# Attention weights kept by key block and multiplied with V once per pair of heads; the memory normalised next to the last pair

## The chip, the core and the metric

The kernel runs on one core of one Trainium2 chip. The metric is the device time of one execution in microseconds (us). The engines of the core are named as in the profile: PE (the tensor engine's products), PEld (its weight loads), DVE (the vector engine), ACT (the scalar engine), POOL (GpSimd) and SP (the engine that issues most of the transfers).

## The reference

One layer of a decoder over 512 tokens of width 1024: a projection, two kinds of causal attention with 8 heads of 64 each, an output projection, cross attention to 256 memory tokens, a mixture of 16 experts, and a norm. What matters here:

```python
u = rmsnorm(h)
qA, kA, vA, qB, kB, vB, f = split(u @ w_in)
# FoX: per head, causal softmax with a decay from the forget gates
p = softmax(mask(qA @ kA.T / 8 + c_t - c_s));            oA = p @ vA
# stick-breaking: per head, strictly causal
a = exp(logsigmoid(z) + sum_{s<j<t} logsigmoid(-z_tj));  oB = a @ vB     # z = qB @ kB.T / 8
h = h + concat(rmsnorm(oA), rmsnorm(oB)) @ w_out
kv = rmsnorm(mem) @ w_xkv          # 256 memory tokens
h = h + cross_attention(rmsnorm(h) @ w_xq, kv) @ w_xo
```

## The kernel before

The tokens come last first, so a block of 128 queries sees its own block of keys and those behind it: query block i has 4 - i key blocks, in all 10 blocks of 128 x 128 for a head. Heads are handled in pairs, four pairs for each of the two families: FoX (`fox_pair`, group 0) and stick-breaking (`sb_pair`, group 1). Within a pair, three groups of query blocks, `BLOCKS = ((0,), (1, 3), (2,))`, are gone through head by head.

For each head and group, PE multiplies Q and K (`products`, into the PSUM tile `lg` for FoX, of which there is one, or `Z` for stick-breaking, of which there are two), ACT and DVE make the weights (tiles `p` or `sa`), PE transposes them block by block into the one PSUM tile `tr` (`transposed`), and DVE (FoX) or ACT (stick-breaking, as the exponential) copies `tr` to SBUF as `pT`. When both heads of the group are there, `av` multiplies them with V: for each key block and head one float32 product of 64 columns of V with 128 queries. The two heads write the upper and lower half of the PSUM tile `o`, side by side in the columns of the tensor engine. After the last group `pair_out` copies `o` to its place in `HO` and adds its squares for the norm that follows (`sq`).

The steps of the two families take turns. The projections of the next pair's Q and K (`qk_proj`) and of further V columns (`v_proj`) are written behind the steps of a pair; they read the normalised input as `uh` and `ul`, in three products each (`mm3`). Weights for them come through a ring of three raw tiles, which ACT casts (`wh`) and DVE subtracts from (`wl`). Q and K are then moved into the tiles QQ, KH, KL, QX and KX by transfers on SP.

The order of the instructions on each engine is fixed when the program is built, by a scheduler that moves instructions of later code between those of earlier code where it expects an engine to be free. On the chip each engine goes through its own list in order and waits at semaphores.

The memory (256 tokens) is loaded, normalised (`rms`), transposed and split into `mh` and `ml` (`to_fm`) behind the first V projections, before the first pair; the four rounds of its transpositions rotate over four PSUM tiles (`tr`, `lg` and two `o`). Its keys, products `pj<-mh`, are written behind the last pair, and the scheduler uses them there to fill PE.

Of the kernel before, what the change touches and what calls it, by code (L numbers as in the profile page):

```python
# [11 lines left out]
F32 = mybir.dt.float32  # L12
# [23 lines left out]
FIRST = 4  # L36


def layer(ctx, tc, a, out, dbg=None):
# [24 lines left out]
    # ---------------------------------------------------------------- helpers  # L64
    # a weight unit is 1024 values a partition: loaded whole, then split into two float32r parts
    W = {}

    # the places of a weight's tiles, in turn: (pool, tag count) for the raw unit and for its parts
# [71 lines left out]
    # -------------------------------------------------------------- constants  # L140
# [17 lines left out]
    # ================================================= phase 1: projection, FoX, SB  # L158
# [27 lines left out]
    mp = pool(ckm, "mp", side="left")  # L186
    mh = mp.tile([128, KT, M], F32R, name="mh")
    ml = mp.tile([128, KT, M], F32R, name="ml")
# [13 lines left out]
    # ---- forget gates  # L202
# [20 lines left out]
    # ---- pieces  # L223
# [82 lines left out]
    # what the heads give, by feature: the heads of a pair share a tile  # L306
# [3 lines left out]
    # the tokens come last first: the keys of a query block are its own block and those behind it;  # L310
    # the products of a pair's heads run side by side in the columns of the tensor engine
    def av(o, i, at, pTs, vcol):
        for s in range(i, NT):
            for hh in range(2):
                nc.tensor.matmul(o[hh * HD:(hh + 1) * HD, i * 128:(i + 1) * 128],  # L315
                                 V[:, s, vcol + hh * HD:vcol + (hh + 1) * HD], pTs[hh][:, at + s - i, :],
                                 start=s == i, stop=s == NT - 1)

    def transposed(p, w, copy):
        pt = trp.tile([128, NT, 128], F32, name="tr")  # L320
        for s in range(w // 128):
            nc.tensor.transpose(pt[:, s, :], p[:, s * 128:(s + 1) * 128], ident)  # L322
        pT = wk.tile([128, NT, 128], F32, name="pT", bufs=6)
        copy(pT[:, :w // 128, :], pt[:, :w // 128, :])
        return pT

    # blocks of queries that are handled together
# [16 lines left out]
    # the features of a pair of heads go to their place; their squares are summed over the pairs  # L344
# [9 lines left out]
    def fox_pair(p, ops):  # L354
        o = op_.tile([128, S], F32, name="o4", bufs=2)
# [971 lines left out]
```

## Time and profile before

| | |
|---|---|
| median of 3 runs | 664.81 us (664.63 to 665.65) |
| profiled execution, first to last instruction | 662.1 us |
| PE busy | 625.6 us |
| DVE busy | 461.6 us |
| ACT busy | 376.7 us |
| mean granted clock of PE | 0.990 of full speed |

The span of 662.1 us is that of one profiled execution; the times of the runs hold in addition what lies around the span, some 2.7 us at the median. Busy times of an engine are those of its instructions; matmuls are pipelined, so what a product costs PE is read from the start of one to the start of the next. In the profile of this execution the attention of the four pairs begins at about 69, 112, 177 and 220 us, and two V projections stand between the second and the third pair.

### The profile page before, as it was taken

What the parts mean: (1) busy time and instruction counts of PE and PEld (TensorE: products, weight loads), DVE (VectorE), ACT (ScalarE), POOL (GpSimd) and SP (SyncE); (2) the same over time, 40 slices, a digit from 0 to 9 for tenths busy, and PEclk for the clock granted to TensorE, in tenths of its full rate; (3) what the DMA queues carried; (4) which work ended last, traced back from release to release, by engine and by line L of the source; (5) the groups of instructions that cost most, each with busy time, mean ns of one, the idle gap of its engine ahead of it and who ended that gap; (6) DMA issues with size and microseconds to landing.
All of it is one profiled execution on the core that took longest, in us unless ns stands there. A gap on an engine that the chain in (4) does not pass through costs nothing.

```text
span 662.1 us, 10336 instructions
## 1 busy us (share of the span) xinstructions
PE 625.6 (94%) x3595; PEld 507.4 (77%) x3596; DVE 461.6 (70%) x941; ACT 376.7 (57%) x752; POOL 53.1 (8%) x80
## 2 busy tenths in 40 slices
PE   3999999999999999999999999999999999999980
PEld 2988777888877888988888898867767777777750
DVE  4843794963497797855853466347879999989955
ACT  5632556653456676613632354333369898898842
POOL 2000000000000000000000003000152011010350
PEclk9999999999999999999999999999999999999996
DMA  8545744323764634561453223792989999999494
GB/s 279 171 125 133 186 113 116 92 65 92 171 157 107 169 104 152 200 218 35 121 166 96 77 84 88 260 367 99 313 258 366 378 388 380 386 383 385 130 201 174
DMA packets 105497, 128.91 MB, mean 195 GB/s; under 512 B 8456, under 2 KB 82240, under 8 KB 105440
## 3 DMA queue, kind: packets, MB, share of 16 engines
q1 hardware_dynamic: 101120, 114.43, 54.8%
q0 software_dynamic: 4320, 13.77, 7.6%
q8 instruction: 29, 0.48, 0.3%
q14 instruction: 28, 0.23, 0.1%
HBM read 103.96 MB, written 11.56 MB: 174 GB/s over the span
## 4 chain that ended last, share of the span: by engine, by line
PE 82%; DMA 6%; DVE 4%; ACT 3%; issue 2%; POOL 1%; SPq 1%; DVEq 0%; POOLq 0%
PE pj L136 8%; PE pj L138 8%; PE pj L137 8%; PE o L315 5%; PE gu L136 4%; PE pja L136 4%; PE gu L137 4%; PE gu L138 4%; PE pja L137 4%; PE pja L138 4%; PE tr L322 3%; PE tr L129 3%; PE pjb L137 3%; PE pjb L136 3%; PE pjb L138 3%; PE dn L136 2%
## 5 line engine op out<-in xcount | busy, mean ns | idle before, releaser
L90 DVE TENSOR_TENSOR wl<-w,wh 128x1024 fp32r<-128x1024 f32 (+1 forms) x64 | 78.3, 1223 | 81.3 <-ACT wh L89 75.1
L89 ACT CAST wh<-w 128x1024 fp32r<-128x1024 f32 (+1 forms) x64 | 67.2, 1050 | 104.5 <-PE pj L137 37.3
L709 DVE TENSOR_TENSOR wl<-w,wh 128x512 fp32r<-128x512 f32 x168 | 108.5, 686 | 5.5 <-ACT wh L708 5.1
L708 ACT CAST wh<-w 128x512 fp32r<-128x512 f32 x168 | 96.6, 621 | 12.8 <-PE gu L138 9.8
L136 PE MATMUL pj<-uh,wh 128*128 128x512 f32 x128 | 52.1, 407 | 0.0
L138 PE MATMUL pj<-uh,wl 128*128 128x512 f32 x128 | 51.5, 403 | 0.0
L137 PE MATMUL pj<-ul,wh 128*128 128x512 f32 x128 | 51.2, 400 | 0.0
L136 PE MATMUL gu<-wh,xh 128*128 128x512 f32 x120 | 48.5, 404 | 0.2 <-ACT xh L131 0.2
L138 PE MATMUL gu<-wh,xl 128*128 128x512 f32 x120 | 47.6, 397 | 0.0
L137 PE MATMUL gu<-wl,xh 128*128 128x512 f32 x120 | 47.1, 393 | 0.0
L136 PE MATMUL pj<-wh,uh 128*128 128x256 f32 (+1 forms) x128 | 37.7, 294 | 2.3 <-ACT uh L131 2.3
L138 PE MATMUL pj<-wh,ul 128*128 128x256 f32 (+1 forms) x128 | 37.5, 293 | 0.0
L137 PE MATMUL pj<-wl,uh 128*128 128x256 f32 (+1 forms) x128 | 37.3, 292 | 0.0
L315 PE MATMUL o<-pT,V 128*64 128x128 f32 x320 | 33.0, 284 | 0.1
L136 PE MATMUL pja<-wh,fmh 128*128 128x512 f32 x80 | 32.4, 405 | 0.0
L137 PE MATMUL pja<-wl,fmh 128*128 128x512 f32 x80 | 31.9, 399 | 0.0
L138 PE MATMUL pja<-wh,fml 128*128 128x512 f32 x80 | 31.8, 398 | 0.0
L315 PEld LDWEIGHTS o<-pT,V 128*64 128x64 f32 x320 | 21.4, 136 | 10.0 <-issue 5.2
L136 PEld LDWEIGHTS pj<-uh,wh 128*128 128x128 f32 x128 | 24.1, 188 | 6.3 <-issue 1.7
L138 PEld LDWEIGHTS pj<-uh,wl 128*128 128x128 f32 x128 | 24.1, 188 | 5.9 <-issue 0.9
L368 ACT ACTIVATE p<-lg,nm 128x512 f32<-128x512 f32 (+3 forms) x32 | 16.9, 527 | 20.4 <-DVE nm L366 20.3
L137 PEld LDWEIGHTS pj<-ul,wh 128*128 128x128 f32 x128 | 24.1, 188 | 4.8 <-issue 0.3
(356 smaller groups left out, 1633.2 us busy)
## 6 DMA issues: line engine op xcount, KB each, us to landing
w<-in_w_exp_gate_dram SPq DMA_DIRECT2D x64, 256.0 KB, 7.6
w<-in_w_exp_up_dram SPq DMA_DIRECT2D x64, 256.0 KB, 7.6
w<-in_w_exp_down_dram SPq DMA_DIRECT2D x32, 512.0 KB, 7.6
w<-in_w_in_dram SPq DMA_DIRECT2D x24, 512.0 KB, 4.1
w<-in_w_xkv_dram SPq DMA_DIRECT2D x16, 512.0 KB, 4.4
Y<-y SPq DMA_DIRECT2D x14, 512.0 KB, 8.7
KH<-th SPq DMA_DIRECT2D x32, 128.0 KB, 2.3
w<-in_w_out_dram SPq DMA_DIRECT2D x8, 512.0 KB, 4.3
```

The source lines that it names most:

```text
L89: nc.scalar.copy(h, raw)
L90: nc.vector.tensor_sub(l, raw, h)
L129: nc.tensor.transpose(pt[:, j, :], src[:, k * 128:(k + 1) * 128], ident)
L136: nc.tensor.matmul(o, lh, rh, start=start, stop=False)
L137: nc.tensor.matmul(o, lh, rl, start=False, stop=False)
L138: nc.tensor.matmul(o, ll, rh, start=False, stop=stop)
L315: nc.tensor.matmul(o[hh * HD:(hh + 1) * HD, i * 128:(i + 1) * 128], V[:, s, vcol + hh * HD:vcol + (hh + 1) * HD], pTs[hh][:, at + s - i, : ...
L322: nc.tensor.transpose(pt[:, s, :], p[:, s * 128:(s + 1) * 128], ident)
L368: nc.scalar.activation(p_[:, cs], lg[:, cs], AF.Exp, bias=nm, scale=1.0, accum_out=sm)
L708: nc.scalar.copy(h, raw)
L709: nc.vector.tensor_sub(l, raw, h)
```

## The change

`av` is called once for a pair and family, when all groups of both heads are done. The copies of the transposed weights go into one tile of 15 blocks for each head, in which the query blocks of a key block stand next to each other. `av` then goes through five runs of (key block, first query block, number of query blocks): 384, 128, 384, 256 and 128 columns. The generators leave the weights in `W`, and the loop multiplies both families and calls `pair_out` after the last step of a pair. `pT` gets 4 tiles of 15 blocks instead of 6 of 4 blocks.

The memory's load, norm and transposition become a function that is called behind the projections of the last pair, after the pool of `uh` and `ul` is closed: `mh`, `ml` and the tiles of its norm take the place of `uh` and `ul`. All its transpositions go through `trp`, which has one tile. Its gain is loaded on POOL's queue instead of SP's. Otherwise comments are taken out, which shifts lines.

```diff
+PTS = 4
...
     ckm = ExitStack()
-    mp = pool(ckm, "mp", side="left")
-    mh = mp.tile([128, KT, M], F32R, name="mh")
-    ml = mp.tile([128, KT, M], F32R, name="ml")
     cu = ExitStack()
...
-    def av(o, i, at, pTs, vcol):
-        for s in range(i, NT):
-            for hh in range(2):
-                nc.tensor.matmul(o[hh * HD:(hh + 1) * HD, i * 128:(i + 1) * 128],
-                                 V[:, s, vcol + hh * HD:vcol + (hh + 1) * HD], pTs[hh][:, at + s - i, :],
-                                 start=s == i, stop=s == NT - 1)
-
-    def transposed(p, w, copy):
+    def av(pTs, vcol):
+        o = op_.tile([128, S], F32, name="o4", bufs=2)
+        runs = [(NT - 1, 0, NT - 1, 3 * NT - 3), (NT - 1, NT - 1, 1, 3 * NT + 1)]
+        runs += [(s, 0, s + 1, 3 * s) for s in range(NT - 2, -1, -1)]
+        for n, (s, i, w, at) in enumerate(runs):
+            for hh in (1, 0):
+                nc.tensor.matmul(o[hh * HD:(hh + 1) * HD, i * 128:(i + w) * 128],
+                                 V[:, s, vcol + hh * HD:vcol + (hh + 1) * HD],
+                                 pTs[hh][:, at * 128:(at + w) * 128],
+                                 start=n == 0, stop=n == len(runs) - 1, skip_group_check=True)
+        return o
+
+    def transposed(p, at, w, pT, copy):
         pt = trp.tile([128, NT, 128], F32, name="tr")
         for s in range(w // 128):
             nc.tensor.transpose(pt[:, s, :], p[:, s * 128:(s + 1) * 128], ident)
-        pT = wk.tile([128, NT, 128], F32, name="pT", bufs=6)
-        copy(pT[:, :w // 128, :], pt[:, :w // 128, :])
-        return pT
+        i = at[0][0]
+        n = w // 128
+        dst = pT.rearrange("p (a b q) -> p a b q", b=3, q=128)[:, :, i % 3, :]
+        copy(dst[:, i + i // 3:i + i // 3 + n, :], pt[:, :n, :])
+
+    def weights_by_key():
+        return [wk.tile([128, 15 * 128], F32, name="pT", bufs=PTS) for _ in range(2)]
...
     def fox_pair(p, ops):
-        o = op_.tile([128, S], F32, name="o4", bufs=2)
+        pTs = weights_by_key()
...
-                pTs.append(transposed(p_, w, nc.vector.tensor_copy))
-                if len(pTs) == 1:
-                    yield
-            for i, cs in at:
-                av(o, i, cs.start // 128, pTs, p * 128)
-            yield
-        pair_out(o, 0, p)
+                transposed(p_, at, w, pTs[hh], nc.vector.tensor_copy)
+                yield
+        W["av0"] = pTs
...
-    mark("mem")
-    g_mem = nw.tile([128, D], F32, name="gain", bufs=2)
-    nc.sync.dma_start(g_mem, a["norm_mem"][0].partition_broadcast(128))
-    for t in range(2):
-        xt = nw.tile([128, D], F32, name="mt", bufs=2)
-        nc.sync.dma_start(xt, mem2[t * 128:(t + 1) * 128, :])
-        rms(nw, xt, g_mem, xt, D)
-        to_fm(src, xt, mh, ml, t * 128)
     cn.close()
-    qk = pool(c1, "qk", side="right")
-    wk = pool(c1, "wk", side="right")
+
+    def memory():
+        mp = pool(ckm, "mp", side="left")
+        mh, ml = (mp.tile([128, KT, M], F32R, name=n) for n in ("mh", "ml"))
+        with ExitStack() as cm:
+            mw = pool(cm, "mw", side="left")
+            g_mem = gain_bc(mw, a["norm_mem"][0], D, 1)
+            for t in range(2):
+                xt = mw.tile([128, D], F32, name="mt", bufs=2)
+                nc.sync.dma_start(xt, mem2[t * 128:(t + 1) * 128, :])
+                rms(mw, xt, g_mem, xt, D)
+                to_fm(trp, xt, mh, ml, t * 128)
+        return mh, ml
+
+    ca = ExitStack()
+    qk = pool(ca, "qk", side="right")
+    wk = pool(ca, "wk", side="right")
...
         for c in "sf":
             for _ in steps[c]:
                 pass
+
+        for g in range(2):
+            pair_out(av(W[f"av{g}"], g * 512 + p * 128), g, p)
...
             nb = qk_proj(1, p + 1)
             na = qk_proj(0, p + 1)
-    cu.close()
-
-    # ================================================= memory keys and values
+        if p == 2:
+            cu.close()
+            mh, ml = memory()
+
+    ca.close()
```

The same edit as in `fox_pair` is made in `sb_pair`, with `exp` as the copy and `W["av1"]`.

How the instructions stand on the engines, in the program as it is built (a line, an operation, output <- inputs, the output's size; `x4` is four in a row). First PE at the end of the third pair before, where the last transpositions and V products stand between projection products (`pj<-uh`):

```order
L137 MATMUL pj<-ul,wh 128x512
L138 MATMUL pj<-uh,wl 128x512
L322 MATMUL tr<-ident,sa 128x128 x2
L315 MATMUL o_1978<-pT,V 64x128
L136 MATMUL pj<-uh,wh 128x512
L137 MATMUL pj<-ul,wh 128x512
L315 MATMUL o_1958<-pT,V 64x128 x3
L322 MATMUL tr<-ident,p 128x128 x2
L138 MATMUL pj<-uh,wl 128x512
L136 MATMUL pj<-uh,wh 128x512
L137 MATMUL pj<-ul,wh 128x512
L315 MATMUL o_1978<-pT,V 64x128 x3
```

And PE there in the change, from the last two transpositions on; ahead of them the projection products have run out:

```order
L327 MATMUL tr<-ident,sa 128x128 x2
L327 MATMUL tr<-ident,p 128x128 x2
L318 MATMUL o_2077<-pT,V 64x384 x2
L318 MATMUL o_2077<-pT,V 64x128 x2
L318 MATMUL o_2077<-pT,V 64x384 x2
L318 MATMUL o_2077<-pT,V 64x256 x2
L318 MATMUL o_2077<-pT,V 64x128 x2
L318 MATMUL o_2092<-pT,V 64x384 x2
L318 MATMUL o_2092<-pT,V 64x128 x2
L318 MATMUL o_2092<-pT,V 64x384 x2
L318 MATMUL o_2092<-pT,V 64x256 x2
L318 MATMUL o_2092<-pT,V 64x128 x2
```

The V products of both families have moved from many places into one piece of 20. The second place is PE at the beginning of the last pair. Before, the products with the memory (`pj<-mh`) follow the pair's first Z products directly:

```order
L138 MATMUL pj<-uh,wl 128x512
L341 MATMUL Z<-KH,QQ 128x512
L341 MATMUL Z<-KL,QQ 128x512
L341 MATMUL Z<-KH,QQ 128x512
L341 MATMUL Z<-KL,QQ 128x512
L136 MATMUL pj<-mh,wh 128x256
L137 MATMUL pj<-ml,wh 128x256
L138 MATMUL pj<-mh,wl 128x256
```

In the change these come behind the V products, the logits of the next groups and the transpositions of the memory (`mt`):

```order
L350 MATMUL Z<-KH,QQ 128x384
L350 MATMUL Z<-KL,QQ 128x384
L350 MATMUL Z<-KH,QQ 128x128
L350 MATMUL Z<-KL,QQ 128x128
L130 MATMUL tr<-ident,mt 128x128 x12
L350 MATMUL Z<-KH,QQ 128x256
L350 MATMUL Z<-KL,QQ 128x256
L137 MATMUL pj<-mh,wh 128x256 x2
L130 MATMUL tr<-ident,mt 128x128 x4
L138 MATMUL pj<-ml,wh 128x256
L139 MATMUL pj<-mh,wl 128x256
L350 MATMUL lg<-KH,QQ 128x384
```

The memory's transpositions, which stood before the first pair, now stand between PE and its fill. The third place is ACT at the same point. Before, behind the copies and squares of the third pair's two outputs:

```order
L346 COPY HO<-o_1958 128x512
L351 ACTIVATE sa<-o_1958 128x512
L346 COPY HO<-o_1978 128x512
L351 ACTIVATE sa<-o_1978 128x512
L89 CAST wh<-w 128x1024
L279 CAST th<-pj 128x512
L397 ACTIVATE sa<-Z 128x512
```

And in the change; `junk,ss<-mt` is the memory's sum of squares:

```order
L355 COPY HO<-o_2077 128x512
L360 ACTIVATE sa<-o_2077 128x512
L355 COPY HO<-o_2092 128x512
L360 ACTIVATE sa<-o_2092 128x512
L400 ACTIVATE sa<-Z 128x512
L401 ACTIVATE sa<-sa 128x512
L376 ACTIVATE p,sm<-lg,nm 128x512
L402 ACTIVATE sa<-sa 128x512
L400 ACTIVATE sa<-Z 128x512
L401 ACTIVATE sa<-sa 128x512
L402 ACTIVATE sa<-sa 128x512
L116 ACTIVATE junk,ss<-mt 128x1024
```

The memory's norm has moved in between the first operations of the last pair.

## Rows read from the trace of the kernel before

**Rows 1.** The page, busy time of each engine in us, share of the span, and instructions.

```profile
PE 625.6 (94%) x3595; PEld 507.4 (77%) x3596; DVE 461.6 (70%) x941; ACT 376.7 (57%) x752; POOL 53.1 (8%) x80
```

**Rows 2.** Busy time by stage: the attention of the first pair and of the third, each from its first Z product to its last V product. Start and end, length, then busy us (and instructions) of PE, PEld, DVE, ACT, POOL, the granted clock, and the transfers.

```profile
68.66:108.40 39.74, 39.24 (x237) 28.91 (x235) 32.46 (x72) 24.77 (x52) 0.00 (x0) 1.00 0.56 140
177.40:217.20 39.80, 39.22 (x237) 28.89 (x235) 32.92 (x73) 24.74 (x52) 0.00 (x0) 1.00 0.57 137
```

**Rows 3.** The line of the V products: records, duration in ns (least, median, most), first and last start.

```profile
L315 PE MATMUL o<-pT,V x320: 272/273/324, 76.1 to 259.9; 128*64 128x128 f32 x160
```

**Rows 4.** PE in order of time in the first pair's attention: start, duration, line, operation, count.

```profile
81.58 0.43 PE L315 MATMUL o<-pT,V 128*64 128x128 f32 x2
81.94 0.50 PE L136 MATMUL pj<-uh,wh 128*128 128x512 f32 x1
82.28 0.39 PE L137 MATMUL pj<-ul,wh 128*128 128x512 f32 x1
82.51 0.40 PE L138 MATMUL pj<-uh,wl 128*128 128x512 f32 x1
82.84 1.09 PE L315 MATMUL o<-pT,V 128*64 128x128 f32 x14
83.86 0.50 PE L136 MATMUL pj<-uh,wh 128*128 128x512 f32 x1
84.19 0.39 PE L137 MATMUL pj<-ul,wh 128*128 128x512 f32 x1
```

**Rows 5.** The chain of work that ended last: start, us on the chain, what. The first of these rows is four transpositions of the memory.

```profile
42.18 0.44 PE tr L129 x4
...
82.91 1.02 PE o L315 x14
...
106.20 0.58 PE o L315 x6
```

**Rows 6.** PE in order of time between the third pair and the last.

```profile
220.07 0.39 PE L138 MATMUL pj<-uh,wl 128*128 128x512 f32 x1
...
221.00 0.39 PE L341 MATMUL Z<-KL,QQ 128*128 128x512 f32 x1
221.23 0.28 PE L136 MATMUL pj<-mh,wh 128*128 128x256 f32 x1
```

**Rows 7.** Instructions of DVE and ACT by line and shape from 220.3 to 240 us (count, busy us, mean ns of one, idle time before them), and two neighbours on DVE in order of time.

```profile
L400 DVE SCALAR_TENSOR_TENSOR sa<-Z,sa 128x512 f32<-128x512 f32 x4 | 2.7, 686 | 0.4 <-ACT sa L399 0.3
L403 DVE TENSOR_TENSOR_SCAN sa<-sa 128x512 f32<-128x512 f32 x2 | 2.4, 1220 | 0.0
L403 DVE TENSOR_TENSOR_SCAN sa<-sa 128x384 f32<-128x384 f32 x2 | 1.9, 948 | 0.0
L404 DVE TENSOR_TENSOR sa<-Z,sa 128x512 f32<-128x512 f32 x3 | 2.1, 684 | 0.0
L395 DVE TENSOR_TENSOR Z<-Z,negs 128x128 f32<-128x128 f32 x6 | 1.7, 286 | 1.9 <-PE Z L341 1.9
L366 DVE TENSOR_REDUCE nm<-lg 128x1 f32<-128x512 f32 x2 | 1.4, 681 | 0.0
L398 ACT ACTIVATE sa<-sa 128x512 f32<-128x512 f32 x4 | 2.5, 631 | 0.1
...
203.59 0.68 DVE L280 TENSOR_TENSOR tl<-pj,th 128x512 fp32r<-128x512 f32 x1
204.19 0.15 DVE L370 RECIPROCAL rs<-sm 128x1 f32<-128x1 f32 x1
```

**Rows 8.** The memory's multiplication by the norm and its remainder `ml` on DVE and its square on ACT, by line and shape from 24 to 48 us, and its transpositions on PE in order of time, from the first to the product behind them.

```profile
L117 DVE SCALAR_TENSOR_TENSOR mt<-mt,rr,gain 128x1024 f32<-128x1024 f32 x2 | 2.6, 1288 | 0.1
L131 DVE TENSOR_TENSOR ml<-o,mh 128x512 fp32r<-128x512 f32 x2 | 1.3, 680 | 0.0
L115 ACT ACTIVATE junk<-mt 128x1024 bf16<-128x1024 f32 x2 | 2.1, 1054 | 0.0
...
42.02 0.60 PE L129 MATMUL tr<-ident,mt 128*128 128x128 f32 x4
...
43.68 0.48 PE L136 MATMUL pj<-uh,wh 128*128 128x512 f32 x1
```

**Rows 9.** Moves of K on SP in order of time at the last pair, and from the issues of transfers (count, KB each, median us to landing) the weights for the memory and the memory itself.

```profile
223.71 1.24 SPq L303 DMA_DIRECT2D KH<-th  x2
...
w<-in_w_xkv_dram SPq DMA_DIRECT2D x16, 512.0 KB, 4.4
mt<-in_mem_dram SPq DMA_DIRECT2D x2, 512.0 KB, 6.3
```

**Rows 10.** PE in order of time near the start, and busy time by stage near the end (columns as in rows 2; the granted clock is the third number from the end).

```profile
15.49 0.41 PE L136 MATMUL pj<-wh,uh 128*128 128x256 f32 x1
15.70 0.41 PE L137 MATMUL pj<-wl,uh 128*128 128x256 f32 x1
...
17.83 0.28 PE L138 MATMUL pj<-wh,ul 128*128 128x256 f32 x1
17.95 0.28 PE L136 MATMUL pj<-wh,uh 128*128 128x256 f32 x1
...
646.00:647.00 1.00, 0.07 (x1) 0.00 (x0) 1.00 (x4) 0.53 (x1) 0.00 (x0) 1.00 0.98 279
650.00:651.00 1.00, 0.00 (x0) 0.00 (x0) 1.00 (x5) 0.05 (x1) 0.00 (x0) 0.50 0.00 0
```

More of the change, by code (lines that the diff above doesn't have):

```diff
@@ L354, in fox_pair @@
     def fox_pair(p, ops):
-        o = op_.tile([128, S], F32, name="o4", bufs=2)
+        pTs = weights_by_key()
         for blocks in BLOCKS:
             at, w = spans(blocks)
-            pTs = []
-            for Q, K in ops:
+            for hh, (Q, K) in enumerate(ops):
                 lg = lgp.tile([128, S], F32, name="lg", bufs=1)
@@ L386, in sb_pair @@
     def sb_pair(p, ops):
-        o = op_.tile([128, S], F32, name="o4", bufs=2)
+        pTs = weights_by_key()
         for blocks in BLOCKS:
             at, w = spans(blocks)
-            pTs = []
-            for Q, K in ops:
+            for hh, (Q, K) in enumerate(ops):
                 z = zp.tile([128, S], F32, name="Z", bufs=2)
@@ L404, in sb_pair @@
                 nc.vector.tensor_sub(c[:, :w], z[:, :w], c[:, :w])
-                pTs.append(transposed(c, w, exp))
-                if len(pTs) == 1:
-                    yield
-            for i, cs in at:
-                av(o, i, cs.start // 128, pTs, 512 + p * 128)
-            yield
-        pair_out(o, 1, p)
+                transposed(c, at, w, pTs[hh], exp)
+                yield
+        W["av1"] = pTs
     cn = ExitStack()
```

## The prediction

> **What bounds the kernel now.** I read the page first, then the busy time of the engines by stage, then the tensor engine's instructions in order of time. The page says that PE is busy for 625.6 of 662.1 us [rows 1]. The stages in which the change works look the same: in the attention of the first and of the third pair, PE is busy 39.24 of 39.74 us and 39.22 of 39.80, and DVE 32.46 and 32.92 [rows 2]. So PE is the bound, a microsecond that PE loses or wins there is one of the kernel, and DVE is not far behind. What PE does per microsecond is read from start to start, since matmuls overlap: a product of 512 columns comes every 0.23 us [rows 4].
>
> **What the V products cost now.** They are 320 records [rows 3], two for each of 160 products. The order of before cuts them into 48 pieces: for each pair, family and block group first one product alone (one head, 2 records), later the remaining 7 (14 records) or 3 (6 records). That is 24 pieces of 2, 16 of 14 and 8 of 6. A piece costs more than its products: around the one at 82.84, PE goes from 82.51 to 84.19, which is 1.68 us with two projection products in it that are worth 0.47, so the piece costs 1.21 [rows 4]. The chain of waits gives it 1.02 and a piece of six 0.58 [rows 5]; entering and leaving thus adds 0.19. A piece of two takes 0.36 (81.58 to 81.94), with its ends 0.55. In all 24 x 0.55 + 16 x 1.21 + 8 x 0.77 = 38.8 us of PE time.
>
> **What they cost after.** The columns that stream are the same. 1.02 less 0.58 is 0.44 us for eight more records, that is 0.11 us for two: the records of the two heads, which sit in different halves of the array's columns, run side by side; one record alone takes 0.11 too, as a transposition does [rows 5]. Walking the new order (widths 384, 128, 384, 256, 128, each for both heads, records starting in order, a head's own one after the other) gives 2.7 us for one family and 5.3 for both, because a narrow product waits behind the other head's wide one. Full overlap would give 4.4, none 8.7. The new order puts all 20 products of a pair in one piece, so with its ends 5.6, and 22.4 us for four pairs. **Gain: 38.8 - 22.4 = 16.4 us**; the bounds are 20 and 2.6. The page "TensorEngine Tiling (Array Packing)" of the Trainium skill (Theoretical Speedup) promises up to 2x for an operand of 64 columns; by it the piece would be 4.6 and the gain 20 us. The present pieces reach 1.75x (seven products in eight steps), so I keep the walk. The copies into the weights by key move as many elements in equal runs of 128, so I cost them at nothing.
>
> **What moving the memory costs.** Before, loads, squares and splits of the memory lie beside projection products, and its 16 transpositions take 1.66 us in a row, in four PSUM tiles, without a wait [rows 8]. After, its tiles lie where uh and ul lay, so nothing of it can start before the last product that reads them; its transpositions share the one `tr` tile; and the key products of the memory (`pj<-mh`), which fill PE from 221.23 on [rows 6], wait for it. I walk this stretch with t = 0 where the last product with uh ends (220.30 before).
>
> - 0 to 4.3: PE has the next pair's four Z products and six transpositions. The last three rounds of these pass through the one `tr` tile, each with a copy by ACT or DVE, and ACT casts a weight unit (1.05) between; the last copy ends at about 4.2.
> - 4.3 to 9.8: the V products. 9.7 to 10.2: the first FoX logits of the last pair.
> - ACT has the results of both families (copy, square, copy, square) ahead of the last pair's first stick-breaking operation; the second copy waits for 9.8, so that operation starts at about 10.9, although its input was there at 1.3. Before, the same order stood there, but PE had products to go on with.
> - From 10.4 DVE has 41 instructions up to the third remainder `ml`: four like L400, scans of 512 x2, 384 and 128, three like L404, three maxima, eight additions of a mask, two multiplications of a memory tile (1.29 each), three `ml` (0.68 each), a sum of squares, and some 3.3 us of scalings and narrow ones. By [rows 7, 8] that is 21.0 us of busy time; neighbours overlap by some 0.08 (0.68 long, 0.60 apart at 203.59), so 18.1, and its waits for PE and ACT bring it to about 19.7. The first memory tile is multiplied at 21.9 to 23.2, the second at 25.5 to 26.8, the third `ml` ends at 30.1. The products with the memory flow from **30.7**.
> - The memory's load is issued behind 13 moves of Q and K on SP at 0.6 us each, which begin at about 2.4 when K is cast: at 10.2, and it lands 4.4 to 6.3 us later [rows 9], 14.6 to 16.5. ACT gets to it at 15.2, so it is nearly hidden.
>
> PE's work in these 30.7 us is Z 0.9, transpositions 0.9 and 1.8, V products 5.6, logits 2.6, memory 0.2: 12.0. **Loss: 18.7 us.** Its bounds: 14 if DVE's instructions follow with no wait and ACT starts 2 us earlier, 22 if load and copies come late.
>
> **Smaller terms.** The stages get shorter for PE by about 9.5 us up to the V products, 39.7 to 30.3, and DVE has 32.5 and 32.9 us of work there [rows 2]. Of the 2 to 2.6 us that this is over, the next pair's Z products and some V projection cover a part: I take 1.5 us for the first pair, 0.7 for the third, nothing for the second (two V projections follow it). Behind 30.7 transpositions of the last pair go through one `tr` tile faster than ACT and DVE empty it: 1.8. Bounds for the three together are 0 and 8.
>
> **The clock.** After 646.1 PE does nothing, and from 650 on the granted clock is 0.50, 1.2 GHz [rows 10]. At the start, after 9 us of waiting, products of 256 columns come every 0.21 us, and only from about 17.8 every 0.12 [rows 10]: 22 products lost some 0.1 us each, about 2 us. In the gap PE works for half a microsecond in every two or three, so I expect the fall and take 2.0 for the time at 1.2 GHz behind it; bounds 0 and 4, since slow transpositions lengthen the chain too.
>
> **The sum.** -16.4 + 18.7 + 1.5 + 0.7 + 1.8 + 2.0 = +8.3. The span of 662.1 becomes 670.4; 2.7 us lie around it (the median of the runs is 664.8), which I leave as they are: **673.1 us**, 1.2% slower. What follows the attention stays bound by PE, so I see nothing that gives it back.
>
> **The rivals.**
> - *The gap is smaller and the gain wins (faster).* The place is between the last V product of the third pair and the first steady memory product. The sum is zero where that product comes at t = 22.4 instead of 30.7. That takes a DVE block of 12 us instead of 20. For it: the order is made by a scheduler that thought it good. Against it: busy times of rows that exist. With the block at 11 us, 1.5 us of other stalls and no fall of the clock: 662 us.
> - *The two meet (no change):* 663.5 to 666.1 us; 0.2% either way (1.3 us) is what a measurement of this kernel can tell from none.
> - *DVE becomes the bound of the attention stages.* Its 32.5 us leave no room where PE needs 30.3. If each of the stages loses 3 us more: 682 us.
> - *Wide products of the two heads do not overlap.* For it: only pieces of 128 columns are in the trace. Gain 2.6 instead of 16.4: 687 us.
> - *PE keeps its clock in the gap.* The page "TensorE: Matmul & The Clock Gate" of the Trainium skill (Why this matters for your kernels) warns of idle gaps between bursts of products, after which the clock is halved; the end of this trace agrees. Without the fall the time is 671 us, inside the likeliest case.
>
> **How the numbers follow.** The long gap, with or without the fall of the clock, 667 to 679 us: 0.62. A small gap, 662: 0.18. No change: 0.06. Attention bound by DVE, 682: 0.09. No overlap, 687: 0.05. So faster by over 0.2% is 0.18, within 0.2% 0.06, slower 0.76. The range of 8 in 10 leaves out the last case and the outer halves of the small gap and of the case bound by DVE: 661 to 682.
>
> **What would show it.** In the profile after, the records of V products stand in four pieces of about 5.6 us. Between the last `pj` product with uh and the first steady run with mh there are about 31 us with PE busy for 12, and DVE busy for nearly 20 at a stretch; PE's transpositions of `mt` wait for DVE. ACT's first operation on the last pair's Z comes right after the second family's square. The granted clock is 0.50 somewhere there. The first and third attention stages lose 1 to 3 us. I am wrong if DVE is idle in the gap, if the gap is under 22 us, if a piece of V products takes over 7 us, or if PE is idle elsewhere for more than 5 us.

## The result and the profile after

The changed kernel takes **671.99 us** in the median (669.14 to 672.53), the kernel before 664.72 beside it: a ratio of 1.0095, with an interval of 1.0067 to 1.0123. It is slower, by about 1%; 673.1 was predicted. The profiled execution is the fastest of the four (669.14 us, a span of 667.5), so the sums below stand for it: 5.4 us more span than before [rows 1]. The spans of the other three are 670.0 to 670.9. In every run with both numbers the time is 1.6 to 1.8 us longer than the span; the 2.7 us named ahead of the prediction also hold that the profiled execution of the kernel before was some 1 us shorter than its median one.

The slices for PE and for its clock on the page before, then the page after, busy time and the same slices; they answer to [rows 1]:

```profile
PE   3999999999999999999999999999999999999980
PEclk9999999999999999999999999999999999999996
...
span 667.5 us, 10023 instructions
PE 616.6 (92%) x3435; PEld 501.1 (75%) x3436; DVE 461.7 (69%) x941; ACT 375.9 (56%) x752; POOL 53.9 (8%) x81
PE   3999999999996698999999999999999999999980
PEclk9999999999998599999999999999999999999996
```

PE is busy for 9 us less than before in a span that is longer. Nearly all of its new idle time lies in two slices, the 13th and 14th (200 to 234 us), and there alone, apart from the end, the clock falls. What PE does with V is now this (the line of the V products, then PE in order of time in the first pair, columns as in [rows 3] and [rows 4]):

```profile
L318 PE MATMUL o<-pT,V x160: 272/379/844, 104.4 to 254.5; 128*64 128x384 f32 x64, 128*64 128x128 f32 x64, 128*64 128x256 f32 x32
...
104.21 0.28 PE L138 MATMUL pj<-wl,uh 128*128 128x256 f32 x1
104.42 4.54 PE L318 MATMUL o<-pT,V 128*64 128x384 f32 x40
108.89 0.66 PE L327 MATMUL tr<-ident,sa 128*128 128x128 f32 x4
```

160 records stand where 320 stood, in four pieces. This one starts at 104.42 and the transposition behind it at 108.89; from start to start, less the neighbours' own steps, the pieces of the first, second and last pair cost 4.6 to 4.7 us of PE, not 5.6. The third pair's piece, in the gap, takes 6.23 us at a lower clock.

The gap in order of time, with t = 0 at 200.82, the end of the last product with uh. First busy time by stage, columns as in [rows 2]; then the rows on which the walk of the prediction turned, from PE, ACT, SP and DVE:

```profile
200.82:204.85 4.03, 2.01 (x12) 1.09 (x10) 3.28 (x8) 2.79 (x7) 0.56 (x1) 1.00 0.73 232
204.85:211.50 6.65, 6.65 (x42) 3.56 (x42) 0.69 (x1) 1.46 (x3) 0.00 (x0) 0.74 0.69 158
211.50:231.62 20.12, 9.21 (x32) 6.98 (x30) 18.45 (x41) 13.88 (x31) 0.83 (x2) 0.62 0.24 79
231.62:240.00 8.38, 8.38 (x62) 7.91 (x61) 7.75 (x23) 5.54 (x14) 0.68 (x1) 0.90 0.08 2
```

```profile
203.90 0.44 PE L327 MATMUL tr<-ident,p 128*128 128x128 f32 x2 [1.50 <-ACT p L380]
...
204.85 6.23 PE L318 MATMUL o<-pT,V 128*64 128x384 f32 x40 [0.52 <-DVE pT L331]
...
208.40 0.59 ACT L355 COPY HO<-o 128x512 f32<-128x512 f32 x1 [4.56 <-PE o L318]
...
211.12 0.59 ACT L355 COPY HO<-o 128x512 f32<-128x512 f32 x1 [1.64 <-PE o L318]
...
212.09 0.60 ACT L400 ACTIVATE sa<-Z 128x512 f32<-128x512 f32 x1
...
216.26 1.04 ACT L116 ACTIVATE junk<-mt 128x1024 bf16<-128x1024 f32 x1
...
211.26 0.99 SPq L463 DMA_DIRECT2D mt<-in_mem_dram  x2
...
222.72 1.27 DVE L118 SCALAR_TENSOR_TENSOR mt<-mt,rr,gain 128x1024 f32<-128x1024 f32 x1
...
226.50 1.27 DVE L118 SCALAR_TENSOR_TENSOR mt<-mt,rr,gain 128x1024 f32<-128x1024 f32 x1
...
230.93 0.69 DVE L132 TENSOR_TENSOR ml<-tr,mh 128x512 fp32r<-128x512 f32 x1 [0.43 <-ACT mh L132]
...
232.44 0.56 PE L138 MATMUL pj<-ml,wh 128*128 128x256 f32 x1
```

From 211.50 to 231.62 DVE is busy for 18.45 of 20.12 us, in 41 instructions, at a granted clock of 0.62, while PE has little to do. In the kernel before the key products stood here, at 221.23, without a break [rows 6]. Read as t, predicted against measured:

| step | predicted | measured |
|---|---|---|
| V products of the third pair | 4.3 to 9.8 | 4.0 to 10.3 |
| first Abs of the last pair on ACT | 10.9 | 11.3 |
| load of the memory issued; first square | 10.2; 15.2 | 10.4; 15.4 |
| first, second memory tile multiplied | 21.9, 25.5 | 21.9, 25.7 |
| third `ml` ends | 30.1 | 30.8 |
| products with the memory flow from | 30.7 | 31.6 |

### The profile page after: what moved, and what is told of

It is laid out like the page before. It is cut to its first block, busy times and chain, and to the rows that moved or that the text cites. A ratio compares the mean times of both kernels' runs of the same rounds, so it can differ in the third digit from the quotient of the medians.

```text
span 667.5 us, 10023 instructions
## 1 busy us (share of the span) xinstructions
PE 616.6 (92%) x3435; PEld 501.1 (75%) x3436; DVE 461.7 (69%) x941; ACT 375.9 (56%) x752; POOL 53.9 (8%) x81
## 4 chain that ended last, share of the span: by engine, by line
PE 75%; DVE 10%; DMA 5%; ACT 4%; issue 2%; POOL 1%; SPq 1%; ACTq 0%; DVEq 0%; POOLq 0%
PE pj L137 7%; PE pj L138 7%; PE pj L139 7%; PE gu L137 4%; PE pja L137 4%; PE gu L138 4%; PE gu L139 4%; PE pja L138 4%; PE pja L139 4%; PE tr L130 4%; PE o L318 3%; PE pjb L138 3%; PE pjb L137 3%; PE pjb L139 3%; PE tr L327 3%
## 5 line engine op out<-in xcount | busy, mean ns | idle before, releaser
L139 PE MATMUL pj<-wh,ul 128*128 128x256 f32 (+1 forms) x128 | 37.7, 294 | 0.0
L137 PEld LDWEIGHTS pj<-wh,uh 128*128 128x128 f32 x128 | 25.3, 198 | 2.8 <-ACT uh L132 2.8
L139 PEld LDWEIGHTS gu<-wh,xl 128*128 128x128 f32 x120 | 22.5, 188 | 5.3 <-issue 0.2
L137 PEld LDWEIGHTS gu<-wh,xh 128*128 128x128 f32 x120 | 22.6, 188 | 5.0 <-ACT xh L132 0.5
```

Of the source, the lines that this page charges most:

```text
L137: nc.tensor.matmul(o, lh, rh, start=start, stop=False)
L139: nc.tensor.matmul(o, ll, rh, start=False, stop=stop)
```

## The experiments

All times are medians; each ratio is against the kernel before on the same chip. Not all experiments ran on one chip, so two kernels are compared by how far each lies from the kernel before beside it; the changed kernel lies 7.3 us above. The last table of this section says where each kernel won and lost.

**1. The memory early, through DRAM.** It separates the two halves of the change by putting the memory's work back to its old place.

```
+ kept = dram.tile([2, 128, KT * M], F32)         # at the old place, behind the first V projections
+ for n in range(2): nc.gpsimd.dma_start(kept[n], parts[n])
...
- rms(mw, xt, g_mem, xt, D); to_fm(trp, xt, mh, ml, t * 128)
+ for n, d in enumerate((mh, ml)): nc.gpsimd.dma_start(d, kept[n])
```

> The changed kernel, with the memory loaded, normalised and transposed at its old place near the start; its two parts are written to DRAM there and read back (2 x 1 MB, issued on POOL's queue) into the space of uh and ul when these are free. My theory: the gap of the changed kernel is the memory's normalisation and transposition in the middle of a DVE-bound stretch, and the merged V products alone save about 20 us (a piece takes 4.6 us in the profile of the changed kernel, not 5.6). The read back is issued at t = 0 (end of the last product with uh) and lands by about t = 10, when the V products and the first logits end, so products with mh flow from t = 10 to 12 instead of 31. Sum: 662.1 - 20.4 + 2.5 (DVE in the three other attention stages) + 2 (last pair) = 646 span, 649 us. Rival: the gap is the stage's own, because with merged V products every attention stage is bound by DVE and ACT, and the memory only lies in it: then PE waits as long for other things and the time stays at 665 to 672. Second rival: 2 MB more of reads come late behind the weights: 655 to 660.

Measured: 669.23 us, 1.0078 (1.0051 to 1.0105), 5.7 us above the kernel before, where 649 us was expected. The products with the memory did flow early, from 214.35 (t = 11.7), as I expected, and yet only some 2 us came of it, and the intervals of the two kernels overlap. The wait had moved; busy time by stage and ACT's copies out of `pj`:

```profile
215.00:230.00 15.00, 14.60 (x115) 13.72 (x115) 14.65 (x29) 10.48 (x19) 0.00 (x0) 1.00 0.42 116
230.00:250.00 20.00, 11.72 (x56) 7.84 (x55) 14.74 (x39) 9.93 (x26) 2.06 (x3) 0.68 0.43 133
```

```profile
253.77 0.58 ACT L355 COPY HO<-o 128x512 f32<-128x512 f32 x1 [1.07 <-PE o L318]
254.74 1.08 ACT L520 CAST kmh<-pj 128x512 fp32r<-128x512 f32 x2
```

PE is full up to 230 and then has nothing left but the last pair. Two of the four units of keys fill the two `pj` tiles, and both copies that empty them stand behind the last results, at 254.74. In the kernel before the copies were spread over the last pair. The tiles `kmh` come from a pool that opens only when the last pair's tiles are given back, since the wide weights have taken the room. That is a price of the change that I had not seen. Experiments 5 and 6 test it.

**2. The memory late, alone.** The kernel before with the function `memory()` of the change and its place, nothing else.

```
- rms(nw, xt, g_mem, xt, D); to_fm(src, xt, mh, ml, t * 128)      # at the old place
+ if p == 2: cu.close(); mh, ml = memory()
```

> The kernel before with the other half of the change alone: the memory is loaded, normalised and transposed next to the last pair, in the space of uh and ul; the V products stay as they were (48 pieces). My theory: a gap like that of the changed kernel, with less PE work in it, since the third pair's V products are already done; DVE and ACT can start on the last pair some 6 us earlier, so products with mh flow from about t = 25 with 6 to 7 us of PE work in it: a loss of 18 us, and 2 to 4 for the clock: 682 to 687 us. Rival: the gap comes from the merged V products, which hold up ACT and DVE; then the loss here is under 8 us, 665 to 673.

Measured: 685.11 us, 1.0327 (1.0304 to 1.035), as expected: 21.6 us lost. DVE's third remainder in order of time, with t = 0 at 217.88 here:

```profile
243.28 0.69 DVE L131 TENSOR_TENSOR ml<-tr,mh 128x512 fp32r<-128x512 f32 x1
```

It ends at t = 26.1. The move of the memory makes the gap by itself, without one wide V product; the rival is out.

**3. Narrow products in one piece.**

```
+ runs = [(s, i + b, 1, at + b) for s, i, w, at in runs for b in range(w)]
+ runs.insert(0, runs.pop(2))    # the latest weights first, all others issued behind them
```

> The changed kernel with its V products cut back into products of 128 columns, as before (80 records a family instead of 20 products of up to 384 columns for both families), but still in one piece for each pair. My theory: the gain comes from 4 pieces instead of 48, not from wider products, since the same columns stream: a piece takes 4.6 to 5.0 us, and the time is that of the changed kernel, 669 to 674 us. Rival: each product has a fixed cost beside its columns and the wide ones save it: 160 products instead of 80, by 0.05 us each 4 us more, by 0.1 us each 8 us more (676 to 680).

Measured: 670.70 us, 1.0108 (1.0086 to 1.013), the time of the changed kernel. The first pair's piece:

```profile
104.06 4.59 PE L321 MATMUL o<-pT,V 128*64 128x128 f32 x80
```

80 records take 4.59 us, 40 wider ones take 4.54. The width of the products is worth nothing here; the gain is that 48 pieces became four, in which the two heads alternate throughout.

**4. One head after the other.**

```
- for n, (s, i, w, at) in enumerate(runs):
-     for hh in (1, 0):
+ for hh in (1, 0):
+     for n, (s, i, w, at) in enumerate(runs):
```

> The changed kernel with the V products of one head all ahead of those of the other, instead of in turn, so that neighbours in the queue sit in the same half of the array's columns. My theory: it is the overlap of the two heads that makes a piece 4.6 us; without it a piece takes 8.7 us at full clock, 16 us more in all: 684 to 690 us (somewhat less if a part lies in the gap). Rival: wide products do not overlap now either, and the piece is short for another reason: no change, 669 to 674 us.

Measured: 679.17 us, 1.0255 (1.0216 to 1.0293), 15.6 us above the kernel before and so 8 more than the changed kernel: slower, as expected, but by half of what I expected. The same piece:

```profile
103.61 7.07 PE L318 MATMUL o<-pT,V 128*64 128x384 f32 x40
```

The same 40 records take 7.07 us instead of 4.54 only because of their order. So it is the overlap of the two heads, but 7.07 is not the 8.7 of no overlap. The single records of this trace say why. In the program the five products of a head stand one after the other. On the chip the first product of the next head starts at 105.175, beside the fourth of the head in front (105.169) and ahead of its fifth (105.601); the same comes at the two other changes of head, at 106.741 and 108.306. So a head costs 1.57 us from start to start, where its ten records alone would take 2.16 (an estimate from steps of 0.32, 0.22 and 0.11 us for 384, 256 and 128 columns). PE did not keep strictly to the order of its list here.

**5 and 6. A place for the keys.** `kmh` and `kml` get a pool of their own that opens ahead of `ca.close()`; only `vmh` and `vml` wait. Experiment 5 adds this to experiment 1, experiment 6 to the changed kernel.

```
  kmp = pool(ckm, "kmp", side="left")        # now ahead of ca.close(): kmh, kml
+ ca.close()
+ kmp = pool(ckm, "kmv", side="left")        # vmh, vml
```

> The kernel that reads the memory's parts back from DRAM (the first experiment), with one more edit: the tiles of the keys (kmh, kml) get a pool of their own that opens beside the last pair, and only the values' tiles (vmh, vml) wait for the space that the last pair's tiles leave. My theory: in the first experiment the products with mh did flow from t = 12, but only two of the four units of keys fit into the two PSUM tiles pj, since ACT's copies into kmh stood behind the last pair (at 254.7); with the place free they flow on, and the 20 us of the V products show: 646 to 652 us. Rival: the last pair is bound by DVE whatever PE does beside it, and the time stays at 665 to 670.

> The changed kernel with that edit alone: a pool of their own for kmh and kml, the memory still normalised next to the last pair. My theory: behind the gap of the changed kernel two of the four units of keys are left for the end, after the last pair; with the place free, a third runs beside the last pair and its waits: 2 to 4 us less than the changed kernel, 667 to 670. The gap stays at 31 us. Rival: nothing waits for that place, 671 to 673.

Measured: experiment 5 takes 660.93 us, 0.9932 (0.9909 to 0.9955), faster than the kernel before; experiment 6 takes 668.67, 1.0055 (1.0033 to 1.0077), 4.1 us above the kernel before and so some 3 less than the changed kernel, as expected, though the intervals of the two overlap. ACT's copies into `kmh` in the changed kernel, and then in experiment 6:

```profile
256.72 1.09 ACT L514 CAST kmh<-pj 128x512 fp32r<-128x512 f32 x2
265.61 0.58 ACT L514 CAST kmh<-pj 128x512 fp32r<-128x512 f32 x1
```

```profile
244.47 0.58 ACT L510 CAST kmh<-pj 128x512 fp32r<-128x512 f32 x1
...
255.02 0.59 ACT L510 CAST kmh<-pj 128x512 fp32r<-128x512 f32 x1
```

The first copy comes 12 us earlier, and the last product of the keys starts at t = 66.1 instead of 69.3. Experiment 5 stays 9 us above the upper end of what I expected. Its busy time by stage, and below it the kernel before from t = 0 on:

```profile
203.00:215.00 12.00, 9.19 (x55) 5.11 (x54) 4.14 (x9) 5.57 (x12) 1.06 (x2) 0.86 0.91 270
215.00:225.00 10.00, 9.78 (x76) 9.12 (x75) 9.46 (x16) 7.58 (x14) 0.00 (x0) 1.00 0.49 134
225.00:235.00 10.00, 9.25 (x75) 8.67 (x74) 9.41 (x26) 6.71 (x14) 1.52 (x2) 1.00 0.08 4
235.00:245.00 10.00, 8.20 (x64) 7.41 (x64) 9.64 (x24) 6.69 (x17) 0.50 (x1) 1.00 0.34 103
...
220.00:230.00 10.00, 9.38 (x70) 8.56 (x69) 8.60 (x13) 7.54 (x13) 0.00 (x0) 1.00 0.57 139
```

DVE has 4.14 us of work in the first 12 us, while the third pair's V products and results pass, and is then full to 245 while PE waits. The rival had half the truth. With the V products at the end of a pair, the last pair needs 56 us from the last product with uh to its last V product (203.2 to 259.4); before, it needed 40 (220.3 to 259.9), and DVE was busy for 8.60 of the first 10. That DVE's late start makes the whole difference is argued, not shown: the third pair's V products lie in the 56 us too. And the last pair is not all. By the table below, experiment 5 is 17.1 us ahead of the kernel before at the last product with uh, 7.1 ahead once the last pair is over, and 0.2 ahead at the end. Directly behind the last pair PE waits for the parts of the next weights, where the kernel before had no wait:

```profile
PE pja L138 <- DVE wl L91: 1.6, 1, 1.6
PE pja L137 <- ACT wh L90: 0.3, 1, 0.3
```

What takes the last 3.5 us, in the experts' stage, stays open.

**7. The memory first on DVE** (with two pools): the last pair's first four steps are issued behind the last `ml`.

```
+ if p == 3 and n < 4: behind.enter_context(tc.issue_after(W["ml"].ins))
```

> The kernel with two pools, with DVE's work on the last pair's first four heads' blocks held behind the memory's last remainder ml, so that DVE multiplies and splits the memory before anything else in the gap. My theory: what makes the gap long is DVE's block of 41 instructions, of which most belong to the last pair; without them in front, the third ml ends at t = 26 instead of 31 (the load still lands at 15 to 16, then a square, a multiplication and three rounds of 2.5 us through the one tr tile), but the last pair starts 15 to 18 us later and is left without cover at its end, so the time is worse: 676 to 684 us. Rival: DVE's order does not matter, the memory's own chain is the gap: third ml still at t = 30 to 31.

**8. The memory's load early** (with two pools).

```
- nc.sync.dma_start(xt, mem2[t * 128:(t + 1) * 128, :])
+ nc.gpsimd.dma_start(xt, mem2[t * 128:(t + 1) * 128, :])
```

> The kernel with two pools, with the load of the memory on POOL's queue, which is empty, instead of SP's, where it stands behind 13 moves of Q and K. My prediction called this load nearly hidden (issued at t = 10.4, landed at 15, ACT gets to it at 15.4). Against that: if it lands at t = 6, while DVE and ACT have nothing to do (DVE is idle from 4.6 to 8.7), the squares and multiplications can go ahead of the last pair's block, and the order of DVE does put them there. Then the third ml ends at t = 17 to 20 instead of 31, and the time is 8 to 12 us less than with two pools alone: 656 to 661. If the load was hidden: no change, 667 to 670.

Measured: experiment 7 takes 672.36 us, 1.0131 (1.01 to 1.0162), 3.7 more than with two pools alone; experiment 8 takes 663.47, 0.9986 (0.9967 to 1.0005), 5.2 less, no longer different from the kernel before. DVE's first multiplication and third `ml` in 7 (t = 0 at 199.93), with DVE's wait ahead of them, then in 8 (200.87):

```profile
215.08 0.15 DVE L104 TENSOR_SCALAR rv<-ss 128x1 f32<-128x1 f32 x1 [3.15 <-ACT junk L116]
...
216.09 1.28 DVE L118 SCALAR_TENSOR_TENSOR mt<-mt,rr,gain 128x1024 f32<-128x1024 f32 x1
...
224.30 0.69 DVE L132 TENSOR_TENSOR ml<-tr,mh 128x512 fp32r<-128x512 f32 x1 [1.82 <-ACT mh L132]
```

```profile
212.51 1.28 DVE L118 SCALAR_TENSOR_TENSOR mt<-mt,rr,gain 128x1024 f32<-128x1024 f32 x1
...
221.19 0.69 DVE L132 TENSOR_TENSOR ml<-tr,mh 128x512 fp32r<-128x512 f32 x1
```

With the memory first, the third `ml` ends at t = 25.1 instead of 30.8, as I expected: the last pair's instructions in front of it cost 5.7 us of the gap. The other 25 are the memory's own chain: DVE waits 3.15 us for ACT's square, and from one `ml` to the next, with one `tr` tile, 2.5 us pass. The last pair pays for the change, and the sum is worse (by less than I expected). With the load early, the multiplication comes at t = 11.6 and the third `ml` ends at 21.0, just outside what I expected, and 5.2 of the expected 8 to 12 us show.

**9 and 10. The next pair's first head ahead of the results.** The first head of both families of a pair runs up to its transposition ahead of the V products of the pair before; 9 on the changed kernel, 10 on experiment 5.

```
+ for c in "sf": next(steps[c])      # logits and elementwise work of the first heads
+ if p: v_products(p - 1)            # av and pair_out, for both families
```

> The changed kernel with one difference in the order: the logits and the elementwise work of the first head of both families of a pair are written ahead of the V products and results (copy, square) of the pair before, up to the transposition. My theory: part of the gap is that ACT holds the results of the third pair ahead of the last pair's first stick-breaking operation (first Abs at t = 11.3 in the changed kernel though its input is there at t = 1), so DVE has nothing to do from t = 4.6 to 8.7 and little until 12; with the first head ahead, Abs comes at t = 1.5 to 3, the third ml at 26 to 28, and the same order helps the other pairs a little: 3 to 5 us less, 667 to 669. Rival: what DVE does earlier it only waits for later, since the memory's load lands at t = 15: no change, 671 to 673.

> The same order in the kernel that reads the memory's parts back from DRAM and has two pools (661 us, 0.7% faster than before). There the products with mh are no longer what PE waits for, and the last pair is bound by DVE from t = 10 on; with DVE started some 5 us earlier I expect 3 to 5 us less up to the experts' stage, of which the end may take back a part, since the last expert's weights come at the same time in all kernels so far (last product of the program at 645.5 in the kernel that is 3.7 us ahead at 481): 656 to 660. Rival: the end is set by the transfers of weights alone: 661.

Measured: experiment 9 takes 671.04 us, 1.0113 (1.0079 to 1.0146), no change against the changed kernel: the rival held. Experiment 10 takes 657.68 us, 0.9911 (0.9896 to 0.9927), as expected: 6.2 us under the kernel before, where experiment 5 lies 3.6 under. The intervals of 5 and 10 overlap, so that this order wins 2 to 3 us there is likely and not certain. The first Abs, the third `ml` and the last pair's V products in 9 (t = 0 at 202.42), then these V products in the changed kernel:

```profile
203.81 0.60 ACT L403 ACTIVATE sa<-Z 128x512 f32<-128x512 f32 x1
...
229.71 0.69 DVE L132 TENSOR_TENSOR ml<-tr,mh 128x512 fp32r<-128x512 f32 x1
...
251.64 4.54 PE L318 MATMUL o<-pT,V 128*64 128x384 f32 x40 [0.52 <-DVE pT L331]
...
250.23 4.54 PE L318 MATMUL o<-pT,V 128*64 128x384 f32 x40
```

In 9 the first Abs comes at t = 1.4 and the third `ml` ends at 28.0, as I said, but the last pair's V products start at t = 49.2, in the changed kernel at 49.4: while the memory stands in the way, DVE's earlier start buys nothing. Experiment 10 beats both kernels. Its last product comes 7.1 us earlier than in the kernel before, so its rival, an end that the weights' transfers alone set, is out. One long wait of PE is left in its last pair, for a move of K:

```profile
PE lg L350 <- DMA KH<-th: 4.7, 1, 4.7
```

The memory's parts are read back at the same time; in experiment 9, which reads nothing back, this wait is 0.7 us. That the read back makes it long was not tried by itself.

**11. The gap filled.** 42 products that nobody reads.

```
+ if at[0][0] == 1 or at[0][0] == 0 and Q[0] is not Q[1]: warm(r, 7)
```

> The changed kernel with 42 products of 512 columns more, in groups of 7, behind logits of the last pair's first blocks, written to a PSUM tile that nobody reads: they fill PE's waits in the gap and change nothing else. My prediction gave the fall of the clock 2.0 us. If that is right the granted clock stays at 1.0 behind t = 12, the transpositions of mt and the products behind the gap run at full speed, and the time is 2 to 3 us less than the changed kernel's in spite of the additions (each group takes 1.6 us in a wait of 2 to 3 us): 668 to 670. Rival: the clock costs nothing since PE waits there anyway: 672 to 674, the additions delay the last pair a little.

Measured: 668.11 us, 1.0063 (1.0049 to 1.0077), as expected: 4.2 us above the kernel before, so some 3 us less than the changed kernel (3.9 by the medians alone). All five runs lie under the four of the changed kernel. Three stretches of the gap in the changed kernel, then in this one (the granted clock is the third number from the end):

```profile
216.00:220.00 4.00, 1.74 (x5) 1.56 (x6) 3.97 (x8) 2.64 (x7) 0.00 (x0) 0.52 0.33 97
220.00:224.00 4.00, 2.08 (x8) 1.87 (x7) 4.00 (x15) 3.32 (x10) 0.00 (x0) 0.50 0.01 2
224.00:228.00 4.00, 2.20 (x8) 1.43 (x8) 3.84 (x8) 2.56 (x5) 0.00 (x0) 0.50 0.00 0
```

```profile
216.00:220.00 4.00, 3.26 (x17) 2.82 (x18) 3.97 (x8) 2.64 (x7) 0.00 (x0) 1.00 0.09 25
220.00:224.00 4.00, 2.81 (x17) 2.19 (x16) 3.93 (x13) 2.72 (x10) 0.00 (x0) 1.00 0.01 2
224.00:228.00 4.00, 2.63 (x15) 1.55 (x13) 3.94 (x8) 1.25 (x4) 0.00 (x0) 1.00 0.02 4
```

In these stretches PE stays at 2.4 GHz with more work, and the kernel is faster. The profiled pair shows less of it, 2.7 us at the memory's values and 0.3 at the end: it sets the slowest of these five executions beside the fastest of the changed kernel's four.

Where each kernel stands: the start of the same product less its start in the kernel before, in us, from the one profiled execution of each.

| kernel | last product with uh | first product of the memory's values in `lg` | first of the experts | last of all |
|---|---|---|---|---|
| changed | -19.5 | +6.2 | +6.2 | +5.4 |
| 1 memory early | -17.6 | +5.6 | +5.6 | +5.2 |
| 2 memory late, alone | -2.4 | +21.4 | +21.4 | +21.3 |
| 3 narrow | -20.1 | +6.8 | +6.9 | +7.0 |
| 4 heads in turn | -15.2 | +16.5 | +16.5 | +15.1 |
| 5 early, two pools | -17.1 | -7.1 | -3.7 | -0.2 |
| 6 two pools | -20.3 | +3.1 | +3.0 | +5.2 |
| 7 memory first | -20.4 | +4.8 | +8.5 | +8.3 |
| 8 load early | -19.4 | -2.1 | -1.9 | -0.9 |
| 9 first head ahead | -17.9 | +8.0 | +8.0 | +7.6 |
| 10 first head ahead, on 5 | -15.5 | -6.8 | -6.8 | -7.1 |
| 11 gap filled | -20.1 | +3.5 | +5.0 | +5.1 |

## Why the prediction came out

The time and the way were right, and most steps held; three terms of the sum were wrong in size, and their errors cancelled in part. The profiled execution adds up to 5.5 us, not 8.3. That the median lies within 1.1 us of the forecast is in part luck: the three other executions are 2.5 to 3.4 us longer than the profiled one, and no term of the sum stood for that.

| term | predicted | in the profile |
|---|---|---|
| V products | -16.4 | -20.2 |
| gap and clock in it | +18.7 + 2.0 | +20.9 |
| stages of the first three pairs | +2.2 | +2.7 |
| last pair behind the gap | +1.8 | +3.8 |
| given back later | 0 | -1.7 |
| sum | +8.3 | +5.5 (the spans: +5.4) |

- **V products, mis-sized.** The step that failed is the walk in which records start in order and a narrow product waits behind the other head's wide one. A piece takes 4.6 us at full clock, the full overlap, not 5.6; 38.8 less four times 4.65 is 20.2 (the three parts of the 38.8 add up to 38.7). The two heads' records start within 0.01 us of each other, equal widths side by side, and in experiment 4 a product even starts ahead of its place in the list. The page "TensorEngine Tiling (Array Packing)" of the Trainium skill (Theoretical Speedup) states up to 2x for an operand of 64 columns, from which the prediction had estimated a piece of 4.6 us; here the trace agrees with it, 4.54 us where the two heads take turns and 7.07 where they do not (experiment 4). I took the present pieces' 1.75x for a property of the engine, and it came from pieces in which one head has three products left and the other four. The count of pieces, not the width, was the right thing to price (experiment 3): by the prediction's own prices the ends of 44 pieces, 0.19 us each, make 8.4 of the 20.2; the other 12 are the time of products that ran without a partner in the other half.
- **The gap held**, to within a microsecond at every step. From t = 0 to 31.6 PE had some 10.7 us of work at full clock; the loss of 20.9 includes the low clock in it. One agreement is luck: the V products end at 10.3 against 9.8 because the piece, priced too long, ran in part at 1.2 GHz. The cause held in the main: experiment 2 makes the gap with the memory's move alone. Experiment 7 says how it is shared, which the prediction did not: 5.7 us are the last pair's instructions in front of the memory's, the rest is the memory's own chain. "Nearly hidden" for the load was true of the wait and misleading as a judgement: it landed when ACT came to it, but with the load ahead of the 13 moves the whole order turns out better by 5.2 us (experiment 8).
- **The first three pairs.** From the first Z product to the end of the last with uh it takes 133.8 us instead of 151.6. 36 pieces of before were worth 29.2, two of after 9.3, and six transpositions (0.65) moved out: 131.1 would be left, so 2.7 were lost. PE's waits for DVE in this stretch are 2.3 us, before 0.8; so 1.5 of the 2.7 are seen to be DVE's, and the rest is not assigned.
- **Behind the gap, another cause and half the size.** I gave 1.8 us to transpositions in one `tr` tile. From 232.4 to 270.1 stand 37.7 us for some 32.5 us of work, 5.2 more, where the last pair of before had 1.4 more; experiment 6 shows what most of the 3.8 was: the keys had no place until the last pair was over, and with a place the last of them comes 3.2 us earlier.
- **The clock.** 2.0 us were predicted, for the time at 1.2 GHz behind the gap. The profile shows the low clock ahead of the gap's end instead: 0.50 from 220 to 233, 1.00 again from 234 on. Filling the gap saves some 3 us, inside the bounds of 0 and 4. The 1.6 us that the V products in the gap lose are not in this (6.22 us in experiment 11 too), so the clock may cost more than 4 in all; no run isolates it. The page "TensorE: Matmul & The Clock Gate" of the Trainium skill (Why this matters for your kernels) warns of idle gaps between bursts of products, after which the clock is halved; the trace agrees in direction (0.50 granted from 220 on, 1.00 with the gap filled).
- **"Nothing gives it back"** was wrong by 1.7 us: 7.1 us at the last product of the keys (263.0 before, 270.1 after) are 6.2 at the first of the values and 5.4 at the end.
- **The rivals.** No overlap is out; so is a small gap (and its price of 662 us comes to 660 by its own terms, -16.4 + 10.0 + 1.5, where 10.0 is 18.7 less the 8.7 us by which DVE's block is shorter). DVE as the bound of attention shows in the first three pairs only within the 2.7 us, but it fills the last pair of experiment 5, where 10 of its 17.1 us go.

## What to carry to other kernels

Count the pieces into which an order cuts a run of products before counting their columns: each piece cost some 0.2 us for its two ends, a product without a partner in the other half ran alone, and the width cost nothing. When one edit needs room, follow every tile that loses its place, the ones that are allocated later too: here the memory cost 21 us, and the keys another 3. A result that is gathered to the end of a stage leaves the next stage's elementwise engine with little work at the change (4.14 us of DVE in 12); write the next stage's first steps ahead of it, once nothing else stands in the way: it gave nothing in experiment 9 and probably 2 to 3 us in experiment 10.

## What the runs showed of the hardware

- Two heads in the two halves of the array's columns overlap throughout where their products alternate: 4.54 us for 40 records, against 7.07 for the same 40 with one head's five products ahead of the other's. Even then the next head's first product starts beside the fourth of the head in front, at 105.175, and ahead of its fifth, at 105.601.
- The clock fell within the third pair's V products, while PE was busy, after waits of 1.5 and 0.5 us just ahead of them (0.74 granted from 204.85 to 211.50). That piece takes 6.2 us instead of 4.6. In experiment 9 it stands directly behind other products and takes 4.54.
- The changed kernel's runs spread from 669.14 (mean granted clock 0.976) to 672.53 (0.971); with the gap filled they spread from 667.61 to 669.04. That the longer runs spent longer at 1.2 GHz fits, but was not tried.
